# A one-core kernel of two transformer blocks: six planning passes, new costs and a slack term set the order of its instructions

## The chip, the cores and the metric

The kernel runs on one core of one Trainium2 chip. The metric is the device time of one execution in microseconds; the figure that counts is the median of the runs shown. Below, PE is TensorE's matmul side and PEld its weight loads, DVE is VectorE, ACT is ScalarE, POOL is GpSimd, SP is SyncE, which here issues the transfers.

## What is computed

One sequence of 256 rows with 1024 columns, in fp32, goes through two blocks. The first block is, with rms_norm around each part:

```python
q, k, v, z, xbc, dt_raw, ga, gs = _split(h @ w_in[l], IN_SIZES)
o_att = stick_breaking_attention(q, k, v)
o_ssm = ssd_branch(z, xbc, dt_raw, conv_w, conv_b, dt_bias, a_log, d_skip, g_ssm_norm)
merged = sigmoid(ga) * (o_att @ w_br_att) + sigmoid(gs) * (o_ssm @ w_br_ssm)
x = x + rms_norm(merged @ w_mix_out, g_post_mix)
x = x + rms_norm(memory_cross_attention(h, mem_n, w_xq, w_xkv, w_xo), g_post_xa)
x = x + rms_norm(swiglu(h, w_gu, w_down), g_post_ffn)
```

The SSD branch (Mamba 2) runs a causal convolution of four taps over `xbc`. The second block has two layers. Each is `x = x + concat(o_mix, o_mem) @ w_out; x = x + conv_ffn(x)`; `o_mix` is an attention with forget gates in layer 0 ("fox") and a low-rank attention with rotary embedding in layer 1 ("MLA"), `o_mem` attends to a memory of 256 rows, and `conv_ffn` has a convolution of three taps between its up and down projections.

## The kernel before

**Tiles and weights.** The 256 rows are two tiles of 128, t = 0 and t = 1. All weights are cut into 615 uses of units, most of 128x1024. A unit is read by one transfer on SP's queue into a raw buffer `wr` (four of them). `prepare` (line 477) then rounds it to fp32r in `wh`, on ACT or as a CAST on DVE, and `prepare_low` (line 493) takes the remainder `wl = wr - wh` by one `tensor_tensor`, on DVE or on POOL. This last operation is called the split of a unit in what follows. Each product with a weight is three matmuls: high by high, high by low, low by high. `proj` does 24 matmuls of up to 256 columns with a unit, `wide_step` six of 512 columns.

**Threads.** The work of each part (a row tile's main path, the attention lanes, the SSD branch, the memory, the angles of the rotary embedding, each split) is a Python generator that yields the next thing it wants: an operation, a weight unit, a bank of PSUM, a buffer. `Program.run` (line 396) looks at all threads, works out the earliest start of each by `start` (line 351), and lets the one with the smallest key go on; so the program's order on every engine is one list, fixed when the kernel is built, and each engine does its part in that order. The key is the start by `Model` (line 181) plus `WT` times the thread's turn. `Model` keeps for each region of memory when it was last written and read and by which engine, a cost for each operation (in `Engine.__getattr__` from its size, for matmuls a number handed to `mm`), and one latency of 0.17 us between any two engines. Where an operation may go to DVE or POOL, the choice is the one that ends first by the model, after a penalty for POOL (`POOL`, 0.8 us, in the SSD stage 0.4).

**Order of the units.** `model_kernel` builds the program twice: once without a chip (`Null`), which gives the order `seen` in which units are first used, and then for good, with units loaded and split in that order.

**Lines in the profile.** All operations of DVE, ACT and POOL come from one lambda and bear line 290; matmuls bear line 539 (`mm`), transposes 543 (`tr`), loads of ACT's function tables 442 (`issue`). So groups are told apart by tiles: `pa` is PSUM, `arena` the fp32 work memory, `arena_r` the one in fp32r, `small` columns of single numbers, `cols` constants. In the changed kernel 290, 539 and 543 become 363, 652 and 656.

## Time and profile before

| what | us |
|---|---|
| median of three runs (lowest, highest) | 1343.54 (1343.25, 1345.54) |
| the profiled execution's own time | 1347.96 |
| its span | 1346.2 |
| PE busy | 1288.8, 96% of the span |
| mean granted clock of TensorE | 0.985 of full speed |

The profiled execution is 4.42 us above the median. The span is what the trace covers; 1.8 us of the execution lie outside it. A row of a timeline shows an instruction (or a run of like ones, with their count), and in brackets how long its engine had been idle just before and whose instruction ended that. The granted clock is 1.00 at 2.4 GHz and 0.50 at 1.2 GHz.

### The profile page before, as it was taken

To read this page: it belongs to the slowest core of one execution; us is meant where nothing else is said; L and a number is where in the kernel's file an instruction comes from. 1 tells how busy PE (TensorE), PEld (TensorE's weight loads), DVE (VectorE), ACT (ScalarE), POOL (GpSimd) and SP (SyncE) were. 2 spreads that over 40 slices of the span, in tenths; PEclk is the share of its full clock that TensorE was granted. 3 is DMA by queue.
4 is the path that set the end of the run, shared out by engine and by line. 5 is a ranking of instruction groups with operands and counts; after the bars stand their busy time and mean duration, and the time that the engine had idled before them with its cause. 6 is when DMAs were issued, how large, how long until landed. Compare 5 with 4: busy or idle time off the path is not lost.

```text
span 1346.2 us, 21976 instructions
## 1 busy us (share of the span) xinstructions
PE 1288.8 (96%) x8332; PEld 1149.1 (85%) x8332; DVE 932.9 (69%) x1474; ACT 802.5 (60%) x1430; POOL 309.3 (23%) x378
## 2 busy tenths in 40 slices
PE   8999999897999999999999899998999989899998
PEld 6989899796888887899997788788999868699997
DVE  6667688897577646755546567798665897686664
ACT  6556577675465656644446556786554776665552
POOL 3153214436122002000005412002111462031110
PEclk8999999998999999999999999999999999899999
DMA  8732634353574633755664333567554333266550
GB/s 292 238 105 85 204 125 139 114 189 119 188 261 148 239 111 114 243 184 184 186 207 152 115 115 121 184 212 234 196 188 137 118 108 108 93 228 198 188 172 32
DMA packets 63322, 221.10 MB, mean 164 GB/s; under 512 B 7536, under 2 KB 7664, under 8 KB 63216
## 3 DMA queue, kind: packets, MB, share of 16 engines
q1 hardware_dynamic: 63216, 219.70, 49.2%
q8 instruction: 65, 1.06, 0.3%
q14 instruction: 41, 0.34, 0.1%
HBM read 218.62 MB, written 1.05 MB: 163 GB/s over the span
## 4 chain that ended last, share of the span: by engine, by line
PE 75%; DVE 12%; POOL 4%; ACT 4%; issue 3%; DMA 2%; SPq 0%; POOLq 0%; DVEq 0%; ACTq 0%
PE pa L539 72%; DVE arena L290 8%; POOL arena L290 3%; PE pa L543 3%; ACT arena L290 2%; DVE wl L290 2%; DVE arena_r L290 1%; ACT wh L290 1%; DMA wr<-in_w_in 1%; POOL small L290 1%; ACT arena_r L290 0%; DMA wr<-in_w_up 0%; POOL wl L290 0%; DMA wr<-in_w_dn 0%; DMA wr<-in_w_br_ssm 0%
## 5 line engine op out<-in xcount | busy, mean ns | idle before, releaser
L539 PE MATMUL pa<-wh,arena_r 128*128 128x512 f32 (+2 forms) x1812 | 590.8, 396 | 5.6 <-ACT wh L290 3.6
L290 ACT ACTIVATE wh<-wr 128x1024 fp32r<-128x1024 f32 (+2 forms) x395 | 407.4, 1043 | 264.4 <-PE pa L539 216.6
L290 DVE TENSOR_TENSOR wl<-wr,wh 128x1024 fp32r<-128x1024 f32 (+2 forms) x341 | 413.0, 1219 | 213.1 <-ACT wh L290 209.1
L539 PE MATMUL pa<-arena_r,wh 128*128 128x256 f32 (+2 forms) x2736 | 498.7, 284 | 1.4 <-DVE arena_r L290 1.4
L539 PEld LDWEIGHTS pa<-arena_r,wh 128*128 128x128 f32 (+2 forms) x2736 | 427.4, 191 | 11.2 <-issue 3.5
L539 PEld LDWEIGHTS pa<-wh,arena_r 128*128 128x128 f32 x1812 | 344.6, 191 | 75.2 <-ACT wh L290 3.8
L539 PE MATMUL pa<-arena_r,wl 128*128 128x256 f32 (+2 forms) x1368 | 387.0, 283 | 0.0
L539 PE MATMUL pa<-wl,arena_r 128*128 128x512 f32 (+2 forms) x906 | 355.5, 392 | 9.4 <-DVE wl L290 9.4
L290 POOL TENSOR_TENSOR wl<-wr,wh 128x1024 fp32r<-128x1024 f32 (+2 forms) x65 | 159.4, 2461 | 586.6 <-ACT wh L290 517.2
L539 PEld LDWEIGHTS pa<-arena_r,wl 128*128 128x128 f32 (+2 forms) x1368 | 261.0, 191 | 0.1
L539 PEld LDWEIGHTS pa<-wl,arena_r 128*128 128x128 f32 x906 | 173.0, 191 | 41.2 <-DVE wl L290 10.6
L290 ACT ACTIVATE arena<-arena 128x512 f32<-128x512 f32 (+5 forms) x130 | 80.6, 626 | 58.4 <-DVE arena L290 56.5
L290 DVE TENSOR_TENSOR arena<-arena 128x512 f32<-128x512 f32 (+4 forms) x117 | 92.8, 808 | 18.0 <-POOL arena L290 8.5
L539 PE MATMUL pa<-arena 128*64 128x128 f32 (+4 forms) x888 | 92.6, 290 | 6.9 <-ACT arena L290 3.2
L539 PEld LDWEIGHTS pa<-arena 128*64 128x64 f32 (+3 forms) x888 | 79.2, 163 | 20.2 <-issue 6.0
L543 PE MATMUL pa<-ident,arena 128*128 128x128 f32 (+3 forms) x446 | 65.9, 279 | 19.8 <-DVE arena L290 10.1
L290 ACT ACTIVATE arena<-pa 128x512 f32<-128x512 f32 (+3 forms) x96 | 52.4, 555 | 50.0 <-PE pa L539 33.1
L290 DVE SCALAR_TENSOR_TENSOR arena<-arena,cols 128x128 f32<-128x128 f32 (+3 forms) x152 | 77.0, 535 | 6.7 <-ACT arena L290 5.3
L543 PEld LDWEIGHTS pa<-ident,arena 128*128 128x128 f32 (+3 forms) x446 | 51.8, 138 | 34.2 <-DVE arena L290 12.2
L290 POOL TENSOR_SCALAR small<-small 128x1 f32<-128x1 f32 x38 | 14.6, 385 | 263.1 <-ACT arena L290 190.3
L290 DVE SCALAR_TENSOR_TENSOR arena<-pa,cols,arena 128x255 f32<-128x255 f32 (+1 forms) x136 | 57.7, 477 | 23.9 <-ACT arena L290 22.6
L290 ACT ACTIVATE arena<-pa,small 128x128 f32<-128x128 f32 (+3 forms) x142 | 54.1, 443 | 30.9 <-PE pa L539 30.6
(128 smaller groups left out, 808.6 us busy)
## 6 DMA issues: line engine op xcount, KB each, us to landing
wr<-in_w_up SPq DMA_DIRECT2D x96, 512.0 KB, 4.0
wr<-in_w_in SPq DMA_DIRECT2D x80, 512.0 KB, 4.3
wr<-in_w_gu SPq DMA_DIRECT2D x44, 512.0 KB, 4.2
wr<-in_w_dn SPq DMA_DIRECT2D x44, 512.0 KB, 4.2
wr<-in_w_down SPq DMA_DIRECT2D x22, 512.0 KB, 3.8
wr<-in_w_fox SPq DMA_DIRECT2D x20, 512.0 KB, 3.7
wr<-in_w_br_ssm SPq DMA_DIRECT2D x16, 512.0 KB, 4.5
wr<-in_w_xkv SPq DMA_DIRECT2D x16, 512.0 KB, 4.3
```

Of the source, the lines that this page charges most:

```text
L290: emit = (lambda: f(*a, **k)) if f else (lambda: None)
L539: self.T.matmul(out, l, r, start=start, stop=stop, skip_group_check=True)
L543: self.T.transpose(out, in_, self.const["ident"][:k, :k])
```

## The change

The selection of the next thread moves from `run` into `next` and is weighed by one more term. Five things differ.

- Costs: matmuls are priced by `Model.product` from their shape, operations of the other engines by new formulas, transfers by 380 in place of 360 bytes a nanosecond and 1.9 in place of 1.5 us after it.
- Latencies: one for each engine in place of 0.17 for all.
- A port: DVE operations with two inputs in SBUF (or one large one, from SBUF to SBUF) and POOL operations with an input exclude each other in the model.
- PE's state: after a gap of more than 2.8 us the model makes matmuls 1.9 times as dear for 3 us.
- Passes: after the first plan six more are built without emitting; each takes the order of units of its predecessor and its due times, which `latest` finds by a backward walk over the operations that the predecessor logged. In `next` an operation's slack (due time less start), cut to -15 to 10 us, is added to its key with weight 0.02. The plan whose last matmul ends first by the model is built for good.

```diff
-    LAT = 0.17
+    LAT = {"PE": 0.205, "DVE": 0.118, "ACT": 0.136, "POOL": 0.06, "DMA": 0.0}
+    USE = {"PE": 0.02, "DVE": 0.0, "ACT": 0.0, "POOL": 0.05, "DMA": 0.1}
+    OWN = {"PE": 0.0, "DVE": 0.118, "ACT": 0.136, "POOL": 0.03, "DMA": 0.0}
...
+                k = int(a[2 * i + 1, lo + j])
+                x = x[j] + ((0.0 if i else self.own[eng]) if k == eng else self.lat[k] + self.use[eng])
...
+    def product(l, r):
+        m, n = Model.region(l)[3], Model.region(r)[3]
+        if l.dtype == F32:
+            return 0.115 if m <= 64 and n == 128 else 2 * max(0.111, n / 1200 + 0.0025)
+        return max(0.06, n / 2400 + (0.0135 if m > 32 else 0.0067))
...
-    def regs(self, eng, cost, outs, ins):
+    def regs(self, eng, cost, outs, ins, port=False):
         i = self.index[eng]
-        e = self.t[eng] = max(self.t[eng], self.deps(eng, outs, ins)) + cost
+        s = max(self.t[eng], self.deps(eng, outs, ins), self.port if port else 0.0)
+        if eng == "PE":
+            self.idle += s - self.t[eng]
+            if s - self.t[eng] > 2.8:
+                self.cold = s + 3.0
+            if s < self.cold:
+                cost *= 1.9
+        e = self.t[eng] = s + cost
+        self.log.append((i, s - self.idle, cost, outs, ins, self.who))
+        if port:
+            self.port = e
         if eng == "DMA":
-            e += 1.5
+            e += 1.9
...
+    def latest(self):
+        due = {}
+        nw, nr = {}, {}
+        inf = 1e9
+        def place(d, t):
+            if t not in d:
+                d[t] = np.full(ARENA // 8 + 1, inf)
+            return d[t]
+        end = max(x[1] + x[2] for x in self.log)
+        for i, s, cost, outs, ins, who in reversed(self.log):
+            f = end
+            for t, lo, hi in outs:
+                f = min(f, place(nr, t)[lo:hi].min() - self.lat[i], place(nw, t)[lo:hi].min())
+            for t, lo, hi in ins:
+                f = min(f, place(nw, t)[lo:hi].min())
+            if i == self.index["DMA"]:
+                f -= 1.9
+            b = f - cost
+            if i == 0:
+                b = min(b, s)
+            for t, lo, hi in outs:
+                place(nr, t)[lo:hi] = inf
+                place(nw, t)[lo:hi] = b
+            for t, lo, hi in ins:
+                x = place(nr, t)[lo:hi]
+                np.minimum(x, b - self.use[i], out=x)
+            due[who] = min(b, due.get(who, inf))
+        return due
...
-            psum = any(x.tensor.name.startswith("pa") for x in [out] + ins)
+            space = lambda x: x.tensor.name.startswith("pa")
+            psum = any(space(x) for x in [out] + ins)
             small = sum(size(x) == 1 for x in ins)
+            big = [x for x in ins if size(x) > 1]
+            port = False
             if eng == "ACT":
-                c = 0.00083 * n + 0.08 + 0.09 * small + (0.15 if len(outs) > 1 else 0)
+                c = 0.00083 * n + (0.07 if psum else 0.11) + 0.08 * small + (0.187 if len(outs) > 1 else 0)
             elif eng == "DVE":
-                one = len([x for x in ins if size(x) > 1]) < 2 and op != "tensor_reduce"
-                c = (0.00052 if one and not psum else 0.00104) * n + 0.07 + 0.05 * (small > 0)
+                one = len(big) < 2 and op != "tensor_reduce"
+                port = sum(not space(x) for x in big) > 1 or one and not psum and n > 32
+                c = (0.00052 if one and not psum else 0.00104) * n + 0.075 + 0.05 * (small > 0)
                 if op == "reciprocal":
                     c = 0.006 * n + 0.1
             else:
-                c = 0.0021 * n + 0.1
+                port = bool(ins)
+                c = 0.0023 * n + 0.25
                 if k.get("op") == OP.pow:
-                    c = 0.165 * n + 0.3
-                if op == "affine_select":
-                    c = 0.001 * n + 0.1
+                    c = 0.165 * n + 0.45
+                elif op == "affine_select":
+                    c = 0.00145 * n + 0.1
+                elif op == "tensor_copy":
+                    c = 0.001 * n + 0.19
+                elif op == "memset":
+                    c = 0.0009 * n + 0.07
...
+    def next(self):
+        best = fit = None
+        can = []
+        for i, t in enumerate(self.threads):
+            s = self.start(t)
+            if s is None:
+                continue
+            end = s
+            if isinstance(t.want, list):
+                p = t.turn() if callable(t.turn) else t.turn
+                eng = t.pick.eng
+                end += t.pick.cost
+                if t.pick.func and SETS.get(t.pick.func, self.table) != self.table:
+                    p += self.cfg["SWITCH"]
+                    end += 1.29
+                key = (s + self.cfg["WT"] * p, p, i)
+            else:
+                p, eng = t.prio, "PE"
+                end += 0.2
+                key = (s + self.cfg["WP"] * p, p, i)
+            if best is None or key < best[0]:
+                best = (key, t)
+            if s >= 0 and (fit is None or end < fit[0]):
+                fit = (end, eng)
+            can.append((s, eng, key, t))
+        if best is None:
+            raise RuntimeError("no thread can go on")
+        if self.due is None or best[0][0] < -0.5 or fit is None:
+            return best[1]
+        best = None
+        for s, x, key, t in can:
+            if isinstance(t.want, list):
+                d = self.due.get(t.who())
+                if d is not None:
+                    d -= s - self.model.idle
+                    key = (key[0] + DUE * min(max(d, DMIN), DMAX),) + key[1:]
+            if best is None or key < best[0]:
+                best = (key, t)
+        return best[1]
...
+            self.cur.name = ("high", key)
             yield o
+            self.cur.name = None
             parts[i] = False
-            self.spawn(self.prepare_low(i, key, H, L, raw, parts), 0, lambda i=i: self.urgency(i))
+            self.spawn(self.prepare_low(i, key, H, L, raw, parts), 0, lambda i=i: self.urgency(i), ("low", key))
...
-                self.mm(out, xh, H[:, kk, :], k == 0, False, c)
+                self.mm(out, xh, H[:, kk, :], k == 0, False)
...
+PASSES = 6
+DUE, DMIN, DMAX = 0.02, -15.0, 10.0
...
-        first = Program(tc, d, out, ar, arr, pa, hl, raw, const, None)
-        first.build()
-        p = Program(tc, d, out, ar, arr, pa, hl, raw, const, first.seen)
+        a = (tc, d, out, ar, arr, pa, hl, raw, const)
+        p = Program(*a, None)
+        p.build()
+        order, due, best = p.seen, None, None
+        for _ in range(PASSES):
+            p = Program(*a, order, due, False)
+            try:
+                p.build()
+            except RuntimeError:
+                break
+            x = (p.model.t["PE"], order, due)
+            if best is None or x[0] < best[0]:
+                best = x
+            order, due = p.seen, p.model.latest()
+        p = Program(*a, *best[1:])
```

All other edits hand these arguments on or drop the cost from calls of `mm`.

The number of matmuls, of transfers and of bytes is the same in both programs. Counted over the whole program, splits of 128x1024 go from 328 on DVE and 62 on POOL to 379 and 11, and loads of function tables on ACT from 23 to 27. Of the splits of the SSD branch (the units used between 202 and 339 us in the trace) 14 were on DVE and 20 on POOL, and now 32 are on DVE and one on POOL. Three places:

DVE, in the SSD branch, at the angles of the rotary embedding (the operations on 128x32; `wl` rows are splits). Before:

```order
L290 SCALAR_TENSOR_TENSOR arena<-arena,cols 128x254
L290 TENSOR_SCALAR arena<-arena 128x32
L290 SCALAR_TENSOR_TENSOR arena<-arena,cols 128x253
L290 TENSOR_SCALAR arena<-arena 128x32
L290 SCALAR_TENSOR_TENSOR arena<-arena 128x32 x3
L290 TENSOR_SCALAR arena<-arena 128x32 x2
L290 TENSOR_TENSOR wl_76<-wr_83,wh_75 128x1024
L290 TENSOR_SCALAR arena<-arena 128x32 x2
L290 SCALAR_TENSOR_TENSOR arena<-arena 128x32 x3
L290 TENSOR_SCALAR arena<-arena 128x32 x2
L290 TENSOR_TENSOR wl_82<-wr_85,wh_81 128x1024
```

and now:

```order
L363 TENSOR_TENSOR wl_64<-wr_86,wh_63 128x1024
L363 TENSOR_TENSOR wl_82<-wr_83,wh_81 128x1024
L363 TENSOR_TENSOR wl_66<-wr_84,wh_65 128x1024
L363 SCALAR_TENSOR_TENSOR arena_r<-arena,cols,arena_r 128x2x128
L363 TENSOR_TENSOR wl_68<-wr_85,wh_67 128x1024
L363 TENSOR_TENSOR arena<-pa,arena 128x512
L363 SCALAR_TENSOR_TENSOR arena<-arena,cols,pa 128x128 x6
L363 TENSOR_SCALAR arena<-arena 128x32
L363 TENSOR_TENSOR arena<-arena 128x512
L363 TENSOR_SCALAR arena<-arena 128x32
L363 SCALAR_TENSOR_TENSOR arena<-arena,cols,pa 128x128
L363 SCALAR_TENSOR_TENSOR arena<-arena 128x32
```

The angles stood in one block with splits behind them; now four splits stand ahead of the first, and the angles are spread between operations of the projections.

POOL at the same place (`small` rows are the reciprocal roots of the norms, the row with x32 is the angles' part on POOL). Before:

```order
L290 TENSOR_TENSOR wl_66<-wr_83,wh_65 128x1024
L290 TENSOR_TENSOR wl_80<-wr_84,wh_79 128x1024
L290 TENSOR_TENSOR wl_76<-wr_85,wh_75 128x1024
L290 TENSOR_TENSOR wl_82<-wr_83,wh_81 128x1024
L290 TENSOR_TENSOR wl_66<-wr_85,wh_65 128x1024
L290 TENSOR_TENSOR wl_80<-wr_86,wh_79 128x1024
L290 TENSOR_SCALAR small<-small 128x1
L290 TENSOR_TENSOR small<-small,mhalf 128x1
L290 TENSOR_SCALAR small<-small 128x1
L290 TENSOR_TENSOR small<-small,mhalf 128x1
L290 TENSOR_SCALAR arena<-arena 128x1 x32
L290 TENSOR_SCALAR small<-small 128x1
```

and now:

```order
L363 TENSOR_TENSOR wl_72<-wr_86,wh_71 128x1024
L363 TENSOR_TENSOR wl_82<-wr_84,wh_81 128x1024
L363 TENSOR_SCALAR small<-small 128x1
L363 TENSOR_TENSOR small<-small,mhalf 128x1
L363 TENSOR_SCALAR small<-small 128x1
L363 TENSOR_TENSOR small<-small,mhalf 128x1
L363 TENSOR_SCALAR small<-small 128x1 x2
L363 TENSOR_TENSOR small<-small,mhalf 128x1 x2
L363 TENSOR_SCALAR small<-small 128x1 x2
L363 TENSOR_TENSOR small<-small,mhalf 128x1 x2
L363 TENSOR_SCALAR arena<-arena 128x1 x32
L363 TENSOR_SCALAR small<-small 128x1 x2
```

Six splits in a row stood ahead of the norms and the angles; two are left.

PE at the start of layer 0 (`ident` rows are transposes of the normalized input, the rows with 12x128 are the projection to the twelve forget gates, the others are 512-column steps of six matmuls). Before:

```order
L539 MATMUL pa<-wh_75,arena_r 128x512
L539 MATMUL pa<-wl_76,arena_r 128x512
L539 MATMUL pa<-wh_75,arena_r 128x512 x2
L539 MATMUL pa<-wl_76,arena_r 128x512
L539 MATMUL pa<-wh_75,arena_r 128x512
L543 MATMUL pa<-ident,arena 128x128 x8
L539 MATMUL pa<-arena_r,wh_73 12x128
L539 MATMUL pa<-arena_r,wl_74 12x128
L539 MATMUL pa<-arena_r,wh_73 12x128 x2
```

and now (of the four units between, the steps in the middle are left out):

```order
L652 MATMUL pa<-wh_79,arena_r 128x512 x2
L652 MATMUL pa<-wl_80,arena_r 128x512
L652 MATMUL pa<-wh_79,arena_r 128x512
L656 MATMUL pa<-ident,arena 128x128 x8
L652 MATMUL pa<-wh_69,arena_r 128x512
L652 MATMUL pa<-wl_70,arena_r 128x512
...
L652 MATMUL pa<-wh_63,arena_r 128x512 x2
L652 MATMUL pa<-wl_64,arena_r 128x512
L652 MATMUL pa<-wh_63,arena_r 128x512
L652 MATMUL pa<-arena_r,wh_77 12x128
```

The gates' projection followed the transposes at once; now four units of the memory's key and value projection, twelve matmuls each, stand between. Two others: the eight transposes of tile 1 at the start of layer 0's feed-forward part follow the last output projection directly, where two steps of the down projection stood between; and at the start of layer 1's feed-forward part one step of the up projection more stands ahead of the transposes, and no split between the two halves of the residual addition.

## Rows read from the trace of the kernel before

**Rows 1.** The page, part 1: busy time of each engine, its share of the span, and the number of instructions.

```profile
PE 1288.8 (96%) x8332; PEld 1149.1 (85%) x8332; DVE 932.9 (69%) x1474; ACT 802.5 (60%) x1430; POOL 309.3 (23%) x378
```

**Rows 2.** Busy time by stretch (the windows view): start and end, length, busy time of PE, PEld, DVE, ACT and POOL (with instructions), mean granted clock, DMA share, GB/s. The stretches are the SSD branch of the first block (w_br_ssm and the last of w_in), the rest of the first block (its output, the memory attention, the SwiGLU part), the start of the feed-forward part of the forget-gate layer, and the MLA layer up to the start of its feed-forward part.

```profile
202.00:339.00 137.00, 122.74 (x906) 111.92 (x907) 115.59 (x186) 87.54 (x180) 66.23 (x68) 0.96 0.42 143
339.00:714.00 375.00, 371.86 (x2215) 330.49 (x2214) 220.09 (x270) 199.90 (x312) 33.48 (x36) 1.00 0.57 187
...
860.00:927.00 67.00, 60.00 (x332) 51.06 (x331) 62.31 (x105) 53.33 (x91) 12.47 (x11) 1.00 0.66 217
...
1060.00:1178.00 118.00, 106.41 (x640) 87.69 (x639) 96.58 (x212) 85.27 (x203) 40.97 (x57) 0.96 0.32 107
```

**Rows 3.** PE's longest waits from 155 us on (timeline of PE): start, length, operation, count, and in brackets the idle time just before and what ended it.

```profile
169.00 1.22 PE L539 MATMUL pa<-arena 128*128 128x128 f32 x4 [2.65 <-ACT arena L290]
...
243.61 0.37 PE L539 MATMUL pa<-negmaskT,identb 128*128 128x256 bf16 x1 [3.13 <-ACT arena L290]
...
268.99 0.66 PE L543 MATMUL pa<-ident,arena 128*128 128x128 f32 x4 [2.79 <-ACT arena L290]
...
317.34 0.80 PE L539 MATMUL pa<-wl,arena_r 128*128 128x512 f32 x1 [5.49 <-DVE wl L290]
...
331.11 2.40 PE L539 MATMUL pa<-arena 128*64 128x128 f32 x40 [1.60 <-DVE arena L290]
...
715.96 0.29 PE L539 MATMUL pa<-arena_r,wh 128*12 128x128 f32 x2 [1.40 <-DVE arena_r L290]
...
739.62 0.39 PE L539 MATMUL pa<-small,triu 128*128 128x12 f32 x2 [1.87 <-POOL small L290]
...
771.87 0.39 PE L539 MATMUL pa<-small,triu 128*128 128x12 f32 x2 [1.97 <-POOL small L290]
...
879.41 1.09 PE L543 MATMUL pa<-ident,arena 128*128 128x128 f32 x8 [2.60 <-DVE arena L290]
...
924.50 0.50 PE L539 MATMUL pa<-wl,arena_r 128*128 128x512 f32 x1 [3.40 <-DVE wl L290]
...
1099.36 0.66 PE L543 MATMUL pa<-ident,arena 128*128 128x128 f32 x4 [2.15 <-DVE arena L290]
...
1163.29 1.97 PE L543 MATMUL pa<-ident,arena 128*128 128x128 f32 x8 [5.62 <-ACT arena L290]
```

**Rows 4.** The windows view again, of short stretches in which TensorE's granted clock was half; columns as in the second group.

```profile
168.40:171.80 3.40, 2.80 (x13) 2.80 (x14) 1.65 (x3) 2.44 (x3) 0.88 (x1) 0.51 0.45 154
243.50:246.90 3.40, 3.29 (x16) 3.29 (x16) 2.96 (x7) 2.83 (x12) 0.93 (x2) 0.51 0.03 11
315.20:322.00 6.80, 4.66 (x11) 3.74 (x12) 6.49 (x14) 3.38 (x7) 3.51 (x4) 0.50 0.53 193
718.00:721.40 3.40, 3.40 (x9) 2.65 (x9) 2.11 (x3) 3.40 (x6) 1.27 (x3) 0.50 0.02 5
...
772.60:776.00 3.40, 3.40 (x9) 2.66 (x9) 1.85 (x2) 0.10 (x1) 3.40 (x9) 0.50 0.69 219
1100.30:1103.70 3.40, 3.40 (x19) 2.45 (x19) 3.29 (x10) 2.20 (x5) 1.36 (x4) 0.50 0.00 0
```

**Rows 5.** Groups of instructions by exact shape (lines by form): line, engine, operation, output and inputs, count | busy us, mean ns of one | idle time before them and what ended it.

```profile
L290 DVE TENSOR_TENSOR wl<-wr,wh 128x1024 fp32r<-128x1024 f32 x328 | 402.6, 1235 | 207.3 <-ACT wh L290 203.3
...
L290 POOL TENSOR_TENSOR wl<-wr,wh 128x1024 fp32r<-128x1024 f32 x62 | 155.6, 2520 | 417.5 <-ACT wh L290 348.2 <-PE pa L539 37.1 <-DVE wl L290 29.1
...
L290 DVE SCALAR_TENSOR_TENSOR arena<-pa,cols,arena 128x255 f32<-128x255 f32 x68 | 31.0, 476 | 22.8 <-ACT arena L290 22.6
...
L442 ACT ACT_TABLE_LOAD x22 | 28.2, 1283 | 0.4
```

**Rows 6.** Timelines of DVE and of POOL at DVE operations that run beside a split on POOL; columns as in the third group.

```profile
158.70 9.10 DVE L290 SCALAR_TENSOR_TENSOR arena<-arena,cols 128x255 f32<-128x255 f32 x12 [0.18 <-ACT arena L290]
...
228.46 12.27 POOL L290 TENSOR_TENSOR wl<-wr,wh 128x1024 fp32r<-128x1024 f32 x5
...
238.55 3.11 DVE L290 SCALAR_TENSOR_TENSOR arena_r<-arena,cols,arena_r 128x128 fp32r<-128x128 f32 x4
...
258.78 9.00 DVE L290 SCALAR_TENSOR_TENSOR arena<-arena,cols 128x255 f32<-128x255 f32 x9
...
325.88 4.48 DVE L290 SCALAR_TENSOR_TENSOR arena_r<-arena,cols,arena_r 128x256 fp32r<-128x256 f32 x2
...
871.80 2.40 DVE L290 TENSOR_TENSOR arena_r<-arena,arena_r 128x256 fp32r<-128x256 f32 x1 [0.62 <-ACT arena_r L290]
...
910.57 2.22 DVE L290 SCALAR_TENSOR_TENSOR arena<-arena,cols 128x128 f32<-128x128 f32 x1 [0.40 <-ACT arena L290]
...
1095.33 2.00 DVE L290 TENSOR_TENSOR arena<-arena 128x64 f32<-128x64 f32 x1
```

**Rows 7.** Timelines of POOL and of DVE at the angles of the rotary embedding.

```profile
300.89 11.32 POOL L290 TENSOR_SCALAR arena<-arena 128x1 f32<-128x1 f32 x32
...
312.25 0.18 DVE L290 TENSOR_SCALAR arena<-arena 128x32 f32<-128x32 f32 x1 [6.27 <-POOL arena L290]
```

**Rows 8.** Timelines of PE in a unit of the forget-gate layer, and of DVE at the end of an output projection.

```profile
736.45 0.39 PE L539 MATMUL pa<-wl,arena_r 128*128 128x512 f32 x1
736.68 0.61 PE L539 MATMUL pa<-wh,arena_r 128*128 128x512 f32 x2
...
1158.38 1.22 DVE L290 TENSOR_TENSOR wl<-wr,wh 128x1024 fp32r<-128x1024 f32 x1
```

More of the change, by code (lines that the diff above doesn't have):

```diff
@@ L188, in __init__ @@
         self.index = {e: i for i, e in enumerate(self.t)}
+        self.lat = [self.LAT[e] for e in self.t]
+        self.use = [self.USE[e] for e in self.t]
+        self.own = [self.OWN[e] for e in self.t]
+        self.port = self.cold = self.idle = 0.0
         self.s = {}
+        self.log, self.who = [], None
     @staticmethod
@@ L216, in after @@
                 j = x.argmax()
-                x = x[j] + ((SAME if eng and not i else 0.0) if a[2 * i + 1, lo + j] == eng else self.LAT)
+                k = int(a[2 * i + 1, lo + j])
+                x = x[j] + ((0.0 if i else self.own[eng]) if k == eng else self.lat[k] + self.use[eng])
                 if x > e:
@@ L284, in call, with __init__, who @@
             else:
[L285 removed]
+                port = bool(ins)
+                c = 0.0023 * n + 0.25
                 if k.get("op") == OP.pow:
[L287 to L289 removed]
+                    c = 0.165 * n + 0.45
[5 more added lines that the diff above has]
+                    c = 0.0009 * n + 0.07
             emit = (lambda: f(*a, **k)) if f else (lambda: None)
[L291 removed]
+            return Op(eng, emit, c, outs, [x for x in ins if x.tensor.name[:3] != "in_"], port=port)
         return call
 class Thread:
[L298 to L300 removed]
+    def __init__(self, gen, prio, turn, ev, key):
+        self.gen, self.prio, self.turn, self.ev, self.key = gen, prio, turn, ev, key
+        self.n = self.kids = 0
+        self.want, self.unit, self.second, self.name = None, None, False, None
+    def who(self):
+        return self.name or (self.key, self.n)
 class Program:
[L304 to L306 removed]
+    def __init__(self, tc, d, out, ar, arr, pa, hl, raw, const, order, due=None, real=True):
+        self.plan = order is None
+        self.order, self.due, self.d, self.out = order, due, d, out
+        plan = self.plan or not real
         nc = Null() if plan else tc.nc
+        self.cur = None
         self.T, self.Q = nc.tensor, nc.sync
@@ L399, in run @@
         while self.threads:
-            best = None
-            for i, t in enumerate(self.threads):
-                s = self.start(t)
-                if s is None:
-                    continue
-                if isinstance(t.want, list):
-                    p = t.turn() if callable(t.turn) else t.turn
-                    if t.pick.func and SETS.get(t.pick.func, self.table) != self.table:
-                        p += self.cfg["SWITCH"]
-                    key = (s + self.cfg["WT"] * p, p, i)
-                else:
-                    p = t.prio
-                    key = (s + self.cfg["WP"] * p, p, i)
-                if best is None or key < best[0]:
-                    best = (key, t, s)
-            if best is None:
-                raise RuntimeError("no thread can go on")
-            _, t, s = best
+            t = self.next()
             self.cur = t
+            m.who = t.who()
             if isinstance(t.want, list):
@@ L442, in issue @@
                     self.real.preload_act_table_set(s)
-                self.model.t["ACT"] += 1.3
+                self.model.t["ACT"] += 1.29
                 self.table = s
         a.emit()
-        self.model.regs(a.eng, a.cost, a.outs, a.ins)
+        self.model.regs(a.eng, a.cost, a.outs, a.ins, a.port)
     def begin_unit(self, key):
@@ L536, in act, with mm @@
         return o
-    def mm(self, out, l, r, start, stop, cost):
+    def mm(self, out, l, r, start, stop):
         self.T.matmul(out, l, r, start=start, stop=stop, skip_group_check=True)
-        self.model.op("PE", cost, [out], [l, r])
+        self.model.op("PE", Model.product(l, r), [out], [l, r])
     def tr(self, out, in_, k=128):
@@ L549, in dma @@
         n = 4 * 128 * (Model.region(out)[3] if o else 1024)
-        self.model.op("DMA", n / 360e3 + 0.05, o, [])
+        self.model.op("DMA", n / 380e3 + 0.05, o, [])
     def copy(self, out, in_, scale=None):
```

102 lines of the change are left out of this document (50 added, 52 removed).

## Prediction

> **What bounds the kernel now.** The page's busy times come first: PE is busy 1288.8 us of 1346.2, no other engine over 69% [rows 1]. The change leaves PE's matmuls as they are, so it can win only two things: the 57.4 us in which PE is idle, and time in which PE runs at half clock. The busy times by stretch say where these lie [rows 2]. From 339 to 714 us PE idles for 3.1 us of 375: no order of instructions wins anything there. From 202 to 339 us, the SSD branch, it idles for 14.3 of 137, from 860 to 927 for 7.0 of 67, from 1060 to 1178 for 11.6 of 118. PE's waits show that these are a few long ones, each ended by one operation of DVE, ACT or POOL [rows 3]. The clock view shows the second cost: from just before the end of six of those waits the granted clock is 0.50 for 3.4 to 6.8 us [rows 4]; 739.62 and 879.41 have no such stretch.
>
> **What makes PE wait.** Behind most of these waits stands a DVE operation that takes several times its length while POOL does a split. A tap or scale on 255 columns takes 0.476 us when one operand is in PSUM [rows 5]; nine with all operands in SBUF took 9.00 us from 258.78, twelve 9.10 from 158.70, four of 128 columns 3.11 from 238.55 beside POOL's block of five splits (12.27 us), two of 256 columns 4.48, one of 64 columns 2.00 [rows 6]. Taking 0.476 us as the undisturbed price for any of these (too dear for the narrow ones), the excess is 4.7, 3.4, 1.2, 3.5 and 1.5 us. I read it as POOL holding DVE up. The other large wait, 5.49 us at 317.34, has another cause: DVE stood for 6.27 us at an angle operation until POOL was through with 32 tiny ones that took 11.32 us, and the split PE needed was queued behind it [rows 3, 7].
>
> **Edits in the model.** The new costs, latencies, the port, the passes and the slack term emit nothing; they cost only through the order they give. So I price the moves. Durations are those of the profiled execution, which took 1347.96 us, 4.4 above the median of 1343.54; I sum against the former and take 4.4 off.
>
> **1. Splits from POOL to DVE.** 51 fewer on POOL (2.520 us each), 51 more on DVE (1.235 each, 63.0 us) [rows 5]. What they release, each at most the wait behind it: at 169.00 the excess of 3.4 covers all 2.65; at 268.99 4.7 covers 2.79; at 331.11 3.5 covers 1.60; at 1099.36 1.5 of 2.15; at 243.61 1.2 are shown and 3.13 would be all, I take 2.2; at 924.50 one operation of 128 columns took 2.22 where 0.48 is due [rows 6], so 1.7 are shown and 3.40 would be all, I take 2.6 [rows 3]. Sum: 13.3.
>
> **2. The angles.** POOL's 32 now come earlier than DVE's part by about twelve units in the order; twelve units of six matmuls at 0.23 us (736.45 to 736.68 [rows 8]) are 16.6 us, longer than POOL's 11.32 [rows 7]. And four splits stand ahead of DVE's first angle operation. The 5.49 at 317.34 go. On POOL no split is queued behind the 32 but the norms' columns are; they stood there before too.
>
> **3. PE's order.** At 715.96 four units of twelve matmuls (11 us) now stand between the transposes and the product that waited 1.40: gone. At 771.87 the cover grows from eight units to thirteen: 1.97 gone. At 739.62 the work ahead shrinks by some 4 us, so that 1.87 stays and may grow by up to 2; I charge 1.0. At 1163.29 one split of 1.22 between two halves of the residual goes [rows 8] and six matmuls (1.38) cover more: 2.6 of 5.62. At 879.41 twelve matmuls of cover (2.76) are lost; DVE's 2.40 before it [rows 6] shrinks by at most 1.9: between +0.8 and +2.8, I take +1.8. Gained: 1.40 + 1.97 + 2.6 - 1.8 = 4.2.
>
> **4. Clock.** Of the half-clock stretches, those at 168, 243, 315, 718, 772 and 1100 stand at waits that shrink or go. PE is busy 2.80 + 3.29 + 4.66 + 3.40 + 3.40 + 3.40 = 20.95 us in them [rows 4]; at full clock the same work takes half: 10.5 gained. The lengthened wait at 879.41 may bring a new one; I charge 1.7, half of 3.4.
>
> **5. What is given back.** In the SSD branch the moves would take 2.2 + 2.79 + 5.49 + 1.60 = 12.1 of waiting and 4.0 of clock, from 137.0 down to 120.9. But DVE is busy 115.6 there [rows 2], 18 more splits make 22.2, and the excesses shown give back 9.4 (4.7, 1.2, 3.5): 128.4. It cannot be done in 120.9, so 7.5 are returned. That number leans on two errors that pull apart: DVE without any gap (it now idles for 21.4) and only the excesses shown released (POOL's twenty splits there were 50 us). Four more table loads on ACT, 1.283 each [rows 5], cost between nothing (ACT is busy 60% [rows 1]) and 5.1 if PE waits for each; I take 2.6. Below nothing is excluded, they compute nothing. SP's transfers keep number and size; their order follows the units', and no wait in [rows 3] ends with one, so I charge nothing; if their cover failed, the waits would show a DMA.
>
> **Sum.** -13.3 - 5.5 - 4.2 - 10.5 = -33.5; back 7.5 + 1.0 + 1.7 + 2.6 = 12.8. Net -20.7: 1327.3 in a profile like this one, **1322.9** as a median.
>
> **Rivals.** *Nothing is given back*: DVE fits the splits into its idle time, ACT hides the tables. For it: 21.4 us of DVE idle in the SSD branch. Against: they were waits for PE's results. 1347.96 - 33.5 - 4.4 = 1310.
>
> *The waits only move.* A plan made by a model trades one late operation for the next. Then the SSD branch returns all its 16.1, the gains of item 3 with their clock (1.40 + 1.97 + 2.6 + 3.4 = 9.4) turn up at other products, and 1.8 + 1.7 at 879, 2 at 739 and 5.1 for tables are paid. Left are 169.00, 924.50 and 1099.36 with two clock stretches (2.65 + 2.6 + 1.5 + 3.1 = 9.9): -9.9 + 10.6 = +0.7, or 1344. For it: PE is at 96%, with many operations just in time.
>
> *Slower: DVE becomes the bound in the SSD branch.* If the long DVE operations have another cause than POOL, nothing is released and 22.2 us are added to 115.6 busy of 137.0. With no gaps that is 137.8, +0.8; with all the present idle time kept +22.2; I take half, +11.5. From 860 to 927 three more splits meet DVE at 62.3 of 67 [rows 2]: +3.7. Items 1 and 2 vanish; of items 3 and 4 remain 1.40 + 1.97 + 2.6 and the clock at 718 and 772, 3.4. So -9.4 + 11.5 + 3.7 + 1.8 + 1.7 + 1.0 + 2.6 = +12.9, or 1356. It decides once the release plus the idle time that DVE can fill is under 22.2. For it: in the SSD branch DVE is at 84%, nearest to full of all but PE. Against: the excess appears where POOL splits, and the operations on PSUM keep 0.476. The Trainium skill has a rule on this side: "Perfetto Trace Analysis", section "Optimizing Scalar/DVE Operations", says that with DVE saturated it may pay to move work to ACT or even GpSimd. By it this change goes the wrong way and the time is this rival's 1356, against 1323 by the rows. The same section adds that DVE and GpSimd share an SBUF read port, so that moving between those two may not help; the stretched operations of [rows 6] agree, nine times 0.476 having become 9.00. So the rule gets this rival's chance and no more.
>
> That the change doesn't do what it says is small: the order of instructions shows the splits moved and the angles spread. What stays open is whether the chip likes it.
>
> **Chances.** Forecast 0.55 (its own range 1312 to 1333, where 2 to 23 us are given back in place of 12.8), nothing given back 0.17, waits only move 0.16, slower 0.12. A measurement of this kernel can tell about 0.2% (2.7 us) from no change. The first two are faster, of the third nearly half, 0.07, is faster and 0.08 the same, 0.01 and the last are slower: 0.79, 0.08, 0.13. The range takes the forecast's with most of the second and third: 1306 to 1345; out are the slower end and the lowest of the second.
>
> **What would show it.** Right: DVE operations with both inputs in SBUF back near 0.48 us for 255 columns; splits on POOL some 11; no wait of over 3 us left from 202 to 339; mean clock in that stretch above 0.96; DVE there at 120 us or more, nearly full; waits at the fox gates gone at the first and the third place. Wrong: PE waiting in the SSD branch for DVE's splits in many places, or stretched DVE operations without POOL beside them; then the third rival holds. New waits of 2 us or more behind ACT's table loads or at the start of the feed-forward parts would mean the second.

## The result and the profile after

The changed kernel takes 1309.42 us (median of four runs, 1308.68 to 1311.11) beside 1344.01 for the kernel before: ratio 0.9743, 95% interval 0.9726 to 0.9760, or 34.6 us less. The forecast was 1322.9 with a range of 1306 to 1345: the direction and the places were right, the gain was too small, and the time is that of the first rival, 1310, in which nothing is given back. The profiled execution took 1311.11 us.

The page of the kernel after, busy times; they answer to [rows 1]:

```profile
PE 1281.2 (98%) x8332; PEld 1142.1 (87%) x8332; DVE 932.4 (71%) x1519; ACT 810.7 (62%) x1443; POOL 181.2 (14%) x324
```

PE idles for 28.2 us in place of 57.4. DVE is the row to look at: it does 51 more splits of 128x1024, 63 us of work, and is busy for the same time as before, 932.4 against 932.9.

The windows view, cut at the same weight units as before (columns as in [rows 2]; the units of 202.3 to 337.7, 337.7 to 714, 714 to 778, 860 to 928.5 and 1060 to 1178.1 before):

```profile
195.90:316.00 120.10, 117.60 (x903) 107.75 (x902) 104.57 (x177) 90.15 (x180) 21.55 (x48) 1.00 0.45 150
316.00:690.00 374.00, 372.39 (x2214) 331.15 (x2214) 224.50 (x301) 209.00 (x321) 19.70 (x30) 1.00 0.58 193
690.00:744.00 54.00, 52.45 (x287) 43.24 (x286) 38.22 (x70) 36.25 (x78) 30.41 (x65) 1.00 0.46 146
...
826.00:894.80 68.80, 64.37 (x340) 55.02 (x339) 59.99 (x111) 55.45 (x94) 3.77 (x8) 0.95 0.63 212
...
1025.90:1141.40 115.50, 106.79 (x641) 86.24 (x640) 93.90 (x216) 87.74 (x209) 30.45 (x53) 0.99 0.34 113
```

| stage | before, us | after, us | measured | forecast |
|---|---|---|---|---|
| up to the SSD branch | 202.3 | 195.9 | -6.4 | -4.0 |
| SSD branch | 135.4 | 120.1 | -15.3 | -8.6 |
| rest of the first block | 376.3 | 374.0 | -2.3 | 0 |
| start of layer 0 | 64.0 | 54.0 | -10.0 | -5.8 |
| layer 0 up to its feed-forward part | 82.0 | 82.0 | 0 | 0 |
| start of that part | 68.5 | 68.8 | +0.3 | +0.9 |
| the rest of it | 131.5 | 131.1 | -0.4 | 0 |
| layer 1 up to its feed-forward part | 118.1 | 115.5 | -2.6 | -5.8 |
| the rest | 168.1 | 168.0 | -0.1 | 0 |

(Forecast: the terms of the prediction put to their stages; 2.6 us for table loads had no place.) PE's waits of over 1.1 us behind the first 15 us, from its timeline; they answer to [rows 3]:

```profile
296.65 0.66 PE L656 MATMUL pa<-ident,arena 128*128 128x128 f32 x4 [1.49 <-ACT arena L363]
...
718.83 0.39 PE L652 MATMUL pa<-small,triu 128*128 128x12 f32 x2 [1.20 <-POOL small L363]
...
843.85 1.54 PE L656 MATMUL pa<-ident,arena 128*128 128x128 f32 x6 [3.41 <-DVE arena L363]
...
1044.05 0.44 PE L652 MATMUL pa<-wl,arena_r 128*128 128x384 f32 x1 [1.33 <-DVE wl L363]
...
1091.75 2.56 PE L656 MATMUL pa<-ident,arena 128*96 128x128 f32 x13 [1.83 <-DVE arena L363]
```

One is over 2 us, where [rows 3] held eight. In the SSD branch a single one is left, at other transposes. One has grown: the transposes at the start of layer 0's feed-forward part, 2.60 before, 3.41 now. The half-clock stretches from there on (windows view, answering to [rows 4]):

```profile
843.10:849.90 6.80, 6.05 (x19) 5.08 (x20) 6.45 (x17) 6.57 (x15) 0.42 (x3) 0.50 0.23 77
1092.30:1095.70 3.40, 3.40 (x21) 2.91 (x19) 3.40 (x9) 2.84 (x5) 0.00 (x0) 0.50 0.02 6
```

DVE and POOL by shape (lines by form, answering to [rows 5]):

```profile
L363 DVE TENSOR_TENSOR wl<-wr,wh 128x1024 fp32r<-128x1024 f32 x379 | 460.7, 1231 | 174.6 <-ACT wh L363 169.1
L363 DVE TENSOR_TENSOR arena<-arena 128x512 f32<-128x512 f32 x79 | 52.6, 687 | 6.0 <-ACT arena L363 3.2 <-POOL arena L363 0.7
...
L363 DVE SCALAR_TENSOR_TENSOR arena<-pa,cols,arena 128x255 f32<-128x255 f32 x68 | 30.9, 475 | 24.4 <-ACT arena L363 24.3
L363 POOL TENSOR_TENSOR wl<-wr,wh 128x1024 fp32r<-128x1024 f32 x11 | 29.4, 2675 | 113.6 <-ACT wh L363 111.2 <-PE pa L652 2.5
...
L363 DVE SCALAR_TENSOR_TENSOR arena<-arena,cols 128x255 f32<-128x255 f32 x24 | 11.5, 479 | 0.9 <-ACT arena L363 0.8
```

Two of these shapes before (lines by form):

```profile
L290 DVE TENSOR_TENSOR arena<-arena 128x512 f32<-128x512 f32 x79 | 73.1, 944 | 12.9 <-ACT arena L290 6.6 <-POOL arena L290 5.0
...
L290 DVE SCALAR_TENSOR_TENSOR arena<-arena,cols 128x255 f32<-128x255 f32 x24 | 18.4, 771 | 0.9 <-ACT arena L290 0.8
```

The tap on 255 columns with all operands in SBUF took 771 ns on the mean before and takes 479 now; the sum of two 512-column operands took 944 and takes 687. The tap with an operand in PSUM took 476 and takes 475. One shape went the other way: the tap on 253 columns in SBUF took 477 and takes 559, with 11 splits still on POOL.

### The profile page after: what moved, and what is told of

It reads as the page before. It is cut to its first block, busy times and chain, and to the rows that moved or that the text cites. A ratio compares the mean times of both kernels' runs of the same rounds, so it can differ in the third digit from the quotient of the medians.

```text
span 1309.4 us, 21881 instructions
## 1 busy us (share of the span) xinstructions
PE 1281.2 (98%) x8332; PEld 1142.1 (87%) x8332; DVE 932.4 (71%) x1519; ACT 810.7 (62%) x1443; POOL 181.2 (14%) x324
## 4 chain that ended last, share of the span: by engine, by line
PE 85%; DVE 6%; ACT 5%; DMA 2%; issue 1%; POOL 1%; SPq 0%; ACTq 0%; DVEq 0%; POOLq 0%
PE pa L652 82%; DVE arena L363 3%; PE pa L656 3%; ACT arena L363 3%; DVE wl L363 2%; DMA wr<-in_w_in 1%; ACT wh L363 1%; ACT L553 1%; DVE arena_r L363 1%; POOL small L363 1%; DMA arena<-in_mem 1%; DMA wr<-in_w_up 0%; ACT arena_r L363 0%; POOL arena L363 0%; SPq L660 0%
## 5 line engine op out<-in xcount | busy, mean ns | idle before, releaser
L363 DVE TENSOR_TENSOR wl<-wr,wh 128x1024 fp32r<-128x1024 f32 (+1 forms) x395 | 472.6, 1212 | 178.4 <-ACT wh L363 172.9
L652 PEld LDWEIGHTS pa<-wh,arena_r 128*128 128x128 f32 x1812 | 340.9, 189 | 76.1 <-ACT wh L363 4.2
L363 ACT ACTIVATE arena<-arena 128x512 f32<-128x512 f32 (+6 forms) x130 | 80.3, 628 | 31.1 <-DVE arena L363 27.8
L363 ACT ACTIVATE arena<-pa 128x512 f32<-128x512 f32 (+4 forms) x98 | 53.6, 555 | 63.6 <-PE pa L652 38.3
L363 DVE TENSOR_TENSOR arena<-arena 128x512 f32<-128x512 f32 (+4 forms) x117 | 68.2, 601 | 13.3 <-POOL arena L363 5.9
L363 ACT ACTIVATE arena<-pa,small 128x128 f32<-128x128 f32 (+2 forms) x147 | 55.5, 453 | 24.8 <-PE pa L652 24.1
L363 DVE TENSOR_TENSOR arena<-pa,arena 128x512 f32<-128x512 f32 (+3 forms) x74 | 48.9, 670 | 29.1 <-PE pa L652 24.3
L363 DVE SCALAR_TENSOR_TENSOR arena<-arena,cols 128x128 f32<-128x128 f32 (+3 forms) x152 | 59.0, 422 | 6.6 <-ACT arena L363 4.8
```

What stands on the lines that cost most here:

```text
L363: emit = (lambda: f(*a, **k)) if f else (lambda: None)
L652: self.T.matmul(out, l, r, start=start, stop=stop, skip_group_check=True)
```

## The experiments

Ratios are to the kernel before on the same chip, with 95% intervals. Theory 1 is that POOL's splits hold DVE up and that taking them off POOL is worth most of the gain; its rival, that the re-planning with slack made it. The first two kernels exchange engines and keep the order. Each chip has its own time for the kernel before: 1346.1 us beside b_v, a_back, a_pass1 and a_noport, 1347.7 beside a_order, a_slack, a_oldcost and a_nopool, 1347.2 beside the others. So kernels are compared by their ratios, of which 0.01 is 13.4 us on the scale of 1344, and a time in microseconds may be up to 3.7 us too long beside an expectation.

**b_v**

```diff
 o[1].bias = self.cfg["POOL"]
+o[1].emit = o[0].emit
```

> The order of before, word for word, but each of the 65 splits that stood on POOL is issued on DVE at the same place of the list. 62 splits of 1.235 us are 77 us more work on DVE. Theory 1 (POOL's splits hold DVE up, and taking them off POOL is worth most of the gain): DVE's busy time grows by far less than 77 us, by 10 to 25, since the stretched operations return to their short length; the waits of PE at 169, 269, 331, 924 and 1099 us go, those at 317 (angles), 716, 772, 879 and 1163 stay; time 1322 to 1332. Rival (the re-planning with slack made the gain, the engine of the splits is nothing): DVE grows by the whole 77 us and the splits come late behind DVE's other work; time 1343 to 1365.

Measured: 1322.85 us, 0.9828 (0.9807 to 0.9849). Page and lines by form of this kernel:

```profile
PE 1278.9 (97%) x8332; PEld 1142.2 (87%) x8332; DVE 936.6 (71%) x1539; ACT 803.6 (61%) x1430; POOL 156.6 (12%) x313
...
L290 DVE TENSOR_TENSOR wl<-wr,wh 128x1024 fp32r<-128x1024 f32 x390 | 471.8, 1221 | 193.6 <-ACT wh L290 186.9 <-PE pa L540 1.9
...
L290 DVE TENSOR_TENSOR arena<-arena 128x512 f32<-128x512 f32 x79 | 53.1, 689 | 12.8 <-ACT arena L290 6.4 <-POOL arena L290 5.2
...
L290 DVE SCALAR_TENSOR_TENSOR arena<-arena,cols 128x255 f32<-128x255 f32 x24 | 11.4, 476 | 0.1
```

DVE took on 77 us of splits and grew by 3.7, less than the 10 to 25 expected. Its splits of 128x1024 are busy 471.8 us where they were 402.6 [rows 5], so its other work, in the old order, takes 65.5 us less. With nothing else changed, a plan made for other engines gains two thirds of what the change gains. The edit empties POOL's queue as well; but no wait of PE before ends with a split on POOL (waits view), so PE felt POOL's splits through the delay of other engines.

Of the five waits that were to go, those at 269, 331 and 924 are gone (a new one of 1.67 stands at 311.51), but 1.22 of the 2.65 at 169 and 1.48 of the 2.15 at 1099 are left. PE's timeline shows these two and some of those that were to stay:

```profile
168.57 0.94 PE L540 MATMUL pa<-arena 128*128 128x128 f32 x6 [1.22 <-ACT arena L290]
...
241.90 0.27 PE L540 MATMUL pa<-negmaskT,identb 128*128 128x256 bf16 x1 [3.00 <-ACT arena L290]
...
307.01 0.50 PE L540 MATMUL pa<-wl,arena_r 128*128 128x512 f32 x1 [2.66 <-DVE wl L290]
...
752.56 0.39 PE L540 MATMUL pa<-small,triu 128*128 128x12 f32 x2 [1.97 <-POOL small L290]
...
1076.49 0.66 PE L544 MATMUL pa<-ident,arena 128*128 128x128 f32 x4 [1.48 <-DVE arena L290]
...
1138.04 1.97 PE L544 MATMUL pa<-ident,arena 128*128 128x128 f32 x8 [5.62 <-ACT arena L290]
```

At 243.61 the wait stays, now with splits on DVE in the place of the hold. About half of the angles' wait of 5.49 went with the hold: DVE still stands 5.61 us until POOL is through with its 32 (6.27 before [rows 7]), but two angle operations behind that, beside a split on POOL before, are back to their length (timelines of DVE before and in b_v):

```profile
313.62 2.53 DVE L290 TENSOR_SCALAR arena<-arena 128x32 f32<-128x32 f32 x2
...
305.43 0.40 DVE L290 TENSOR_SCALAR arena<-arena 128x32 f32<-128x32 f32 x2
```

The gates' waits and 1163.29 need the new order.

**a_back** (BACK lists the 63 units that before split on POOL and the change on DVE)

```diff
 o[1].bias = self.cfg["POOL"]
+if key in BACK:
+    o[0].emit = o[1].emit
```

> The order of the changed kernel, word for word, but the 63 splits that before did on POOL and the change does on DVE are issued on POOL again at their places. Theory 1: DVE loses some 75 us of splits but is held up again, its busy time falls by 10 to 30 only; PE waits anew in the SSD branch; time 1330 to 1350. Rival (the order alone made the gain): time within 1305 to 1315.

Measured: 1338.99 us, 0.9948 (0.9929 to 0.9967). DVE's busy time did not fall by 10 to 30 us, as I had expected; it rose from 932.4 to 945.7 with 63 splits fewer. Page, and PE's timeline at two places:

```profile
PE 1286.7 (96%) x8332; PEld 1143.5 (86%) x8332; DVE 945.7 (71%) x1456; ACT 810.6 (61%) x1443; POOL 335.6 (25%) x387
...
169.99 1.28 PE L654 MATMUL pa<-arena 128*128 128x128 f32 x6 [4.74 <-ACT arena L363]
...
267.83 1.11 PE L658 MATMUL pa<-ident,arena 128*128 128x128 f32 x4 [4.92 <-ACT arena L363]
```

The two kernels make a square with before and after: the engine is worth 1.7% in the old order and 2.05% in the new, the order 0.5% with splits on POOL and 0.85% without.

At the start of layer 0 the two are not so simply told apart. Windows over the same part of before, b_v and a_back (the change: 54.00 us, 52.45 of PE, above):

```profile
714.00:778.00 64.00, 57.06 (x284) 45.47 (x283) 38.74 (x68) 36.28 (x75) 32.63 (x69) 0.92 0.39 130
...
698.80:757.50 58.70, 52.33 (x283) 41.89 (x282) 37.60 (x69) 36.19 (x74) 29.35 (x68) 1.00 0.39 135
...
712.20:766.70 54.50, 52.52 (x287) 43.28 (x286) 38.74 (x71) 36.43 (x77) 30.61 (x65) 1.00 0.43 145
```

In the new order the stage takes about 54 us wherever the splits run: the order takes PE's idle time there from some 6.5 us to under 2. The rest of the gain is clock, and b_v has it too, with the waits of the old order nearly unchanged.

**a_v** (the edit of b_v in the changed kernel)

> The changed kernel's order, word for word, but the 11 splits left on POOL are issued on DVE at their places. DVE's stretched time left there (some 12 us by the trace) goes, 13.6 us of splits come. If PE waits for any of those places: 1304 to 1308. If not: 1308 to 1311.

Measured: 1309.82 us, 0.9717 (0.9704 to 0.9731): the interval overlaps that of the change. PE's waits of over 1.1 us are the same five as in the change, the first 1.24 in place of 1.49: the last 11 stand where little waits.

**b_ang**

```diff
-yield self.G.tensor_scalar(ang[...], pf[:, t:t + 1], float(inv[j]), None, op0=OP.mult)
+o = [E.tensor_scalar(ang[...], pf[:, t:t + 1], float(inv[j]), None, op0=OP.mult) for E in (self.G, self.V)]
+o[0].emit = o[1].emit
+yield o[0]
```

> The order of before, word for word, but the angles' 32 small products that stood on POOL are issued on DVE at their places, so that nothing on DVE waits for POOL there. If the block of 11.3 us on POOL is the cause of the wait of 5.49 us at 317 and of the half clock behind it: 7 to 8 us less than before, 1336 to 1339 beside a median of 1344. If DVE was late there anyhow from the splits on POOL: 0 to 4 less.

Measured: 1340.92 us, 0.9959 (0.9944 to 0.9974), 5.5 us less (3.5 to 7.5) where 7 to 8 were expected. PE's timeline:

```profile
312.05 0.50 PE L539 MATMUL pa<-wl,arena_r 128*128 128x512 f32 x1 [1.02 <-DVE wl L290]
...
325.79 4.53 PE L539 MATMUL pa<-arena 128*64 128x128 f32 x40 [2.98 <-DVE arena L290]
```

The block was a cause of the wait of 5.49, of which 1.02 is left. A part came back as the next late thing: the wait at 331.11 grew from 1.60 to 2.98, and the half-clock stretch moved there. Windows over the SSD branch and the start of layer 0:

```profile
201.60:335.20 133.60, 121.89 (x899) 111.32 (x899) 119.49 (x219) 88.46 (x179) 59.30 (x36) 0.96 0.43 147
711.60:770.70 59.10, 52.30 (x281) 41.86 (x282) 38.79 (x68) 36.19 (x74) 31.65 (x69) 1.00 0.40 134
```

So in the SSD branch, where the edit stands, this execution wins only some 2 us (133.6 for 135.4). Nearly 5 of the 7.4 us by which its profile is shorter come from the start of layer 0, where nothing was edited: PE waits there much as before (1.40, 1.63, 1.68 and 1.97; the second was 1.87), but the granted clock is 1.00 where it was 0.92. Why it stayed up no run shows. The clock that this stage gave back in b_v and in the change is therefore not shown to be the work of any one wait.

**a_pass1**

```diff
-PASSES = 6
+PASSES = 1
```

> The changed kernel with PASSES = 1: the new costs, latencies and port, but one pass, whose units come in the order of the first plan, and no slack term. Splits on POOL stay few (14). Theory 1: most of the gain stays, 1312 to 1324. Rival (passes and slack make the gain): 1330 to 1345.

Measured: 1330.18 us, 0.988 (0.9861 to 0.9900), at the rival's edge (1328 on the scale of 1344, between the two expectations) and behind b_v. The hold is gone here too (DVE is busy 930.4 us with 14 splits on POOL); time is lost in layer 1 instead, 134.6 us over the matmuls that take 115.7 in the change (PE's timeline, then the window of its longest half-clock stretch):

```profile
1047.01 1.94 PE L656 MATMUL pa<-ident,arena 128*96 128x128 f32 x8 [5.21 <-DVE arena L363]
...
1145.27 1.97 PE L656 MATMUL pa<-ident,arena 128*128 128x128 f32 x8 [5.61 <-ACT arena L363]
...
1044.30:1061.40 17.10, 12.78 (x52) 11.09 (x53) 8.06 (x18) 7.76 (x20) 7.38 (x7) 0.50 0.00 0
```

So theory 1 holds for the engine, and the rival for what comes on top. The next kernels ask what in the planning does that.

**a_noport**

```diff
 self.outs, self.ins = ([Model.region(x)[:3] for x in y] for y in (outs, ins))
+self.port = False
```

> The changed kernel with the port left out of its model: six passes, slack and all new costs stay, but DVE and POOL are planned as if they did not hinder each other. 51 splits go to POOL. Theory 1: DVE operations are stretched again, time 1322 to 1340. Rival (passes, slack and costs make the gain): 1305 to 1316.

Measured: 1333.76 us, 0.99 (0.9877 to 0.9924). Without the port the planner puts 51 splits on POOL in place of 11, and by the ratios 1.6 of the change's 2.6% are lost, some 21 us of 35.

**a_order**

```diff
-p = Program(*a, *best[1:])
+p = Program(*a, best[1])
```

> The changed kernel's units in the order that its chosen plan was given, and its costs and port, but the last building without due times, so without the slack term. If the order of the units that six passes settle on carries the 20 us between one pass and six: 1308 to 1316. If the slack term carries them: 1324 to 1334, with the long waits of the MLA layer (5.5 and 5.8 us in the one-pass kernel) back.

Measured: 1327.45 us, 0.9853 (0.9837 to 0.9869). The waits of layer 1 are back (5.22 at 1050.22).

**a_slack**

```diff
-order, due = p.seen, p.model.latest()
+due = p.model.latest()
```

> The changed kernel with six passes, but each is given the first plan's order of units; only the due times are handed on. If the slack term carries the 20 us: 1308 to 1318. If the re-planned order of units carries them: 1324 to 1334.

Measured: 1328.02 us, 0.9862 (0.9843 to 0.9881). Neither the order of units nor the slack term alone carries the gap between one pass and six, 1.4% or some 18 us: each alone is at most 0.3% better than one pass. The two together do.

**a_oldcost** (costs, latencies and transfer prices of before, no port and no cold state; of the edit, the latencies)

```diff
-LAT = {"PE": 0.205, "DVE": 0.118, "ACT": 0.136, "POOL": 0.06, "DMA": 0.0}
+LAT = {"PE": 0.17, "DVE": 0.17, "ACT": 0.17, "POOL": 0.17, "DMA": 0.17}
...
```

> Six passes and the slack term with the costs, latencies and transfer prices of before and neither port nor cold state (matmuls priced by shape near the old numbers). 54 splits go to POOL. If passes and slack act by themselves: 1322 to 1335, the hold by POOL's splits left as in the kernel without a port (1334). If they only work on top of the fitted costs: 1338 to 1350.

Measured: 1351.83 us, 1.0031 (1.0019 to 1.0043): 4 us slower than before, and 1348 on the scale of 1344, within the second expectation. Passes and slack without the new costs and the port gain nothing. The port is one part of that (a_noport keeps 0.99); which of the other costs makes up the rest is not shown.

**a_nopool**

```diff
-o = [E.tensor_tensor(L, raw, H.bitcast(F32), op=OP.subtract) for E in (self.V, self.G)]
-o[1].bias = self.cfg["POOL"]
-yield o
+yield self.V.tensor_tensor(L, raw, H.bitcast(F32), op=OP.subtract)
```

> The changed kernel, planned with no split on POOL at all (11 there before this edit). If what is left of the hold still costs time: 1300 to 1307. If the 11 stand where nothing waits: 1307 to 1312. If DVE has become the bound where they were: 1312 to 1325.

Measured: 1321.95 us, 0.9811 (0.9794 to 0.9829). The time lies where DVE as the bound would put it, but a_v has the same splits on DVE in the change's own order and loses nothing, and in the SSD branch this kernel is the faster, 117.3 us for 120.1. It is the other plan that costs 0.7%, some 9 us, not the engine.

**a_due15, a_due25** (the weight becomes 0.015 and, in the second, 0.025)

```diff
-DUE, DMIN, DMAX = 0.02, -15.0, 10.0
+DUE, DMIN, DMAX = 0.015, -15.0, 10.0
```

> The changed kernel with the slack's weight at 0.015 in place of 0.020; the plans differ in every stage. If six passes with a slack term find a good plan dependably: 1304 to 1315. If the 13 us by which the change beats the order of before without POOL's splits are one lucky plan of many: 1317 to 1332.

> The changed kernel with the slack's weight at 0.025. As with 0.015: 1304 to 1315 if the method is dependable, 1317 to 1332 if the plan at 0.020 was a lucky one.

Measured: 1315.94 us, 0.9767 (0.9752 to 0.9782), and 1321.09, 0.9802 (0.9785 to 0.9819). The first lies between the two expectations (1313 on the scale of 1344, within the first), the second in that of a lucky plan (1317, its edge). Three weights give 0.974 to 0.980, which is better than planning with one pass, without the slack or without the re-ordering (0.985 to 0.988); 0.6% of the change's 2.6% depends on the weight.

No kernel beat the change by more than the measurement is uncertain.

## Why the prediction was right in kind and short in size

**Step 1, splits from POOL to DVE: right, and the largest term.** The tap on 255 columns came back to 479 ns, PE's waits at 169, 269, 331, 924 and 1099 went, and b_v and a_back show the mechanism by itself: splits on POOL stretch DVE's operations, and PE waits for those. Not every wait was this move's. At 243.61 I credited 2.2 us to it; in b_v, where no split on POOL holds DVE, PE still waits 3.00, besides 1.22 at 169 and 1.48 at 1099. The rest of these went with the new order.

**Step 2, the angles: the wait went as said, its cause was half of it.** POOL's 32 end well before DVE's first angle operation (timelines of POOL and DVE in the kernel after, answering to [rows 7]):

```profile
286.11 14.61 POOL L363 TENSOR_SCALAR arena<-arena 128x1 f32<-128x1 f32 x32 [0.39 <-DVE arena L363]
...
319.11 0.17 DVE L363 TENSOR_SCALAR arena<-arena 128x32 f32<-128x32 f32 x1
```

The 5.49 had two causes, the block on POOL and the hold: b_v keeps the block and halves the wait, b_ang keeps the hold and leaves 1.02. The term and its clock made 7.8 us; b_ang, the block alone, won some 2 in this stage, since the next wait grew and the half clock moved to it.

**Step 3, PE's order: right in direction at four of five places**, and too small at the start of layer 0. There 715.96 and 771.87 went as said and 739.62 shrank to 1.20 where I charged growth; a wait of 1.68 at 750.64 with its half-clock stretch, which I had not listed, went too. 1163.29 is down from 5.62 to two waits of 0.89 and 0.46, 4.3 us where I credited 2.6, and a half-clock stretch there that [rows 4] leave out went with it (windows view, before):

```profile
1161.70:1168.50 6.80, 5.21 (x17) 4.45 (x18) 4.62 (x15) 3.85 (x12) 1.37 (x3) 0.50 0.06 25
```

Yet layer 1 gave 3.2 us less than forecast: at other transposes a wait of 1.83 and a half-clock stretch of 3.40 are new, and so is a wait of 1.33. 879.41 grew by 0.8, at the lower end of what I gave, and brought a half-clock stretch with 6.05 us of PE in it, some 3.0 us where I charged 1.7.

**Step 4, the clock: right in sum, not in place.** Forecast 10.5 less 1.7; PE's busy time, which holds it, fell by 7.6. Of that 4.6 are the start of layer 0, where I had 3.4 and where b_v and b_ang win as much with waits like those of before; in layer 1 the 1.7 did not come.

**Step 5, what is given back: wrong, and the largest part of the miss.** The median fell 13.5 us below the forecast; the profile fell 16.1 below it, since the profiled execution lies 1.7 above its median where I took off 4.4. Of the 16.1 us, 6.7 are the SSD branch, 2.6 the table loads, 4.2 the start of layer 0 (step 3) and 4.7 small waits up to the SSD branch and in the rest of the first block that I had not listed; 1.1 are spread over the rest; layer 1 gave 3.2 less than forecast. I returned 7.5 us in the SSD branch because DVE would need 128.4 us there. It needs 104.6, and the stage takes 120.1, within 1 us of the 120.9 that I had called impossible. The error is mostly the release. I counted it from three groups of operations that stood behind a wait, 9.4 us. But most stretched operations stood behind none, and they held DVE all the same. By shape, their excess over the length in b_v and in the kernel after sums to some 23 us in this stage; one shape (lines by form of the stage, before and after):

```profile
L290 DVE SCALAR_TENSOR_TENSOR arena_r<-arena,cols,arena_r 128x256 fp32r<-128x256 f32 x8 | 9.4, 1178 | 0.0
...
L363 DVE SCALAR_TENSOR_TENSOR arena_r<-arena,cols,arena_r 128x256 fp32r<-128x256 f32 x8 | 3.6, 472 | 0.0
```

Another 8 us or so are operations that the new order does outside the stage, the angles among them: DVE has 177 instructions there after 183, with 19 more splits. Over the program DVE's splits are busy 58.1 us longer (402.6 to 460.7) and its other work 58.6 us shorter. The excess was at hand in the kernel before, in the difference between the mean and the undisturbed length of each shape. The 2.6 us for table loads had no effect on PE that the waits show.

**The rivals.** *Nothing is given back* named the time, 1310, and was right that nothing of the 7.5 us had to be returned in the SSD branch; its reason holds only in part. DVE did not fit them into its idle time: in the SSD branch that time fell from 21.4 to 15.5 us, and most of the room came from the release. That the sum meets the time within 1 us is partly luck: its 33.5 us are 36.9 in the profiles, with some stages above and some below, and the two profiles do not lie equally far above their medians. *The waits only move* came true in two places, at 843.85 and in layer 1, and in b_ang; over the program the eight waits above 2 us became one. *DVE as the bound* is refuted by b_v and by DVE's busy time. The rule that stood for it, the Trainium skill's "Perfetto Trace Analysis", section "Optimizing Scalar/DVE Operations", on moving work from a saturated DVE to GpSimd, points the wrong way here. Its own proviso on the shared read port agrees with a_back: 71 splits on POOL, and 945.7 us of DVE with 63 splits fewer.

**What stays open.** Why the plan at weight 0.020 is better than its neighbours isn't settled: the plans differ in every stage. Over the same numbers of matmuls the kernels at 0.015 and 0.025 lose at the start of layer 0 (57.4 and 57.0 us for 54.1) and in layer 1 (117.8 and 119.2 for 115.7), and 0.025 wins some of it back in the SSD branch. Nor is it shown why the clock at the start of layer 0 fell in the kernel before and stayed up in b_v and b_ang behind like waits.

## What to carry to other kernels

Before moving work between two engines, sum over all shapes how much longer the mean is than the undisturbed length: this is what the receiving engine may get back, and it can be as large as the work that it takes on. A planner's benefit comes from costs that match the trace, contention included; passes and slack on costs that don't match gained nothing. Plans of one planner scatter by half a per cent under small changes of a weight, so one good time of a plan doesn't prove the rule that made it: exchange the suspected piece in a fixed order, and see whether the time went where the piece stands: most of b_ang's gain did not.

## What had not been expected of the hardware

A DVE operation with all operands in SBUF can be drawn out by a split on POOL by nearly the length of the split: 128 columns took 2.22 us [rows 6], where the mean of that shape in the kernel after is 0.348. The mean split on POOL is no shorter where there are fewer: 2553 ns with 71 of them, 2520 with 62, 2675 with 11. And a wait at a bad place costs more than itself: the 5.21 us in layer 1 of a_pass1, and two of 0.77 and 0.84 behind it, stand by 17.1 us at half clock with PE busy for 12.78, of which a full clock would by estimate have saved half. Smaller waits may cost nothing beyond themselves: the four at the start of layer 0, 1.40 to 1.97 us before, stand by three half-clock stretches there, and by none in b_ang, where they are again 1.40 to 1.97.
